# Mixture-of-experts stage: experts ranked on the chip, 14 units of 128 slots in place of 17

## The chip, the cores and the metric

The program runs on one core of one Trainium2 chip. The metric is device time in microseconds, the median over runs. Before the change it is 1516.67 us (three runs, 1516.6 to 1516.83).

## The reference

Two model blocks over 512 tokens of width 1024. The change lies in the first block's mixture of experts alone: a router picks one group of 8 experts for each token, then the two best of these 8. All 32 experts have three weight matrices of their own, 2 MB each in float32.

```python
g_idx = jnp.argmax(g_logits, axis=-1)                      # 4 groups
top_v, top_i = lax.top_k(e_logits, TOP_K_IN_GROUP)         # 2 of the group's 8
wts = g_prob[:, None] * jax.nn.softmax(top_v, axis=-1)
eid = (g_idx[:, None] * EXPERTS_PER_GROUP + top_i).reshape(-1)
...
def expert_block(args):
    tok_b, e = args
    xb = xpad[tok_b]
    h = jax.nn.silu(xb @ w_gate[e]) * (xb @ w_up[e])
    return h @ w_down[e]
```

512 tokens with two experts each are 1024 assignments, 32 for an expert on average. With the reference's inputs the counts of experts 4 to 31, in falling order, are 81, 69, 60, 53, 41, 41, 41, 39, 39, 36, 34, 33, 31, 31, 30, 27 and then twelve from 25 down to 10; experts 0 to 3 have 41, 44, 16 and 16.

## The kernel before

The program is one long instruction list per engine, written out by hand in Python; queues and engines run in the order of the text, with semaphores between them. SP issues nearly all loads, TensorE (PE) multiplies, DVE and ACT evacuate PSUM.

**Units.** The experts' work is cut into 17 units of 128 slots (`pair`, called at the end of the file's main loop, `for p in range(NPAIR + 1)`). A unit normally holds two experts with 64 slots each (`CAP`); each takes a 64-column tile of the PE array, and the two tiles' matmuls alternate (line 77 is the helper `mm`, which nearly all matmuls share). Units 8 and 12 (`DOUBLE`) hold one expert each, on both tiles: the two experts outside the first four with the most assignments, found on the chip. Assignments beyond an expert's slots go to extra units, up to 16 half units, inside a branch (`tc.If(n_more > 0)`, line 1344) after unit 5; with the inputs here the branch is not taken.

**A unit on PE.** Gate weights times gathered tokens, then up weights (`ld,XT`, 32 matmuls in the program; the chip runs float32 as two instructions, so the trace counts 64), then the previous unit's results are spread back to the tokens and added to `h` (`combine`, matmuls `O,oht`, in two halves around four transposes of `ms`), then, in every odd unit, the tokens of the next two units are gathered with one-hot matrices (`gathering`, 64 matmuls `og,hH` and `og,hL`), and then the down weights (`ld,ms`, 16 matmuls, 32 in the trace).

**Loads.** An expert's weights are six tiles `ld` of 1 MB (gate, up and down in two halves), 192 loads in all. `pump` puts them into SP's list as far ahead as the counters allow: at most `at["most"]` weight tiles that are not yet used (16 before the units, then 13, 11, 7 around the branch, 11, 9 for the last four), and 22 slots for all large tiles (`SLOTS`). SP then stands at a load until its slot is given up. From expert 4 on the source address comes from a table `xi` that DVE writes and SP reads into registers (`id_of`).

**Ranking.** `count_more` runs on DVE ahead of unit 0: from the counts `pr` it finds the two biggest experts, gives every assignment its slot `sl` and every place its expert `xi`. Unit 0's SiLU product (line 1061) and the rows `RW` of codes follow it on DVE.

**After the units.** `entering` adds the last unit's results and starts the second block: norm, transposes, and a split of the first weight tile on ACT (line 1267).

Of the kernel before, what the change touches and what calls it, by code (L numbers as in the profile page):

```python
# [20 lines left out]
S, D = 512, 1024  # L21
# [5 lines left out]
NPAIR = NE // 2  # L27
FIXED = 4
MORE = 5
DOUBLE = (8, 12)  # L30
# [3 lines left out]
TWICE = 16384.0  # L34
# [5 lines left out]
def kernel(  # L40
# [679 lines left out]
    places, at_place = {}, 0  # L720
    for p in range(NPAIR + 1):
        if p in DOUBLE:
            places[p] = (NE - 2 + DOUBLE.index(p),)
        else:
            places[p] = (at_place, at_place + 1)
            at_place += 2
        for n in range(3):
            for a in range(2):
                for i in places[p]:
                    jw[n, i, a] = want(partial(weights_of, n, i, a), [128, 4, 512], False)  # L730
# [23 lines left out]
    pcol = small([128, NPAIR + 1 + NEXTRA], "pcol", F32)  # L754
    P.iota(pcol, pattern=[[128, NPAIR + 1 + NEXTRA]], base=0, channel_multiplier=1, allow_small_or_imprecise_dtypes=True)
# [218 lines left out]
    wsl = small([128, 2, NPAIR + 1 + NEXTRA], "wsl")  # L974
# [52 lines left out]
    def pair(p, fetch, last=False, drop=False, own=None, after=None, tail=None):  # L1027

        X = XT[p // 2]
        off = (p % 2) * 128  # L1030
        if own is None:
            pair_codes(p)
        ahead = None
        if p % 2 and p < NPAIR:
            ahead = gathering(p // 2 + 1)
            next(ahead)

        def wfree(ws):
            if p <= NPAIR:
                n = len({id(w) for w in ws.values()})  # L1040
                wlive[0] -= n
                free(*[None] * n)
                pump()

        pg, pu = bank(), bank()
        for n, ps in enumerate((pg, pu)):
            for a in range(2):
                if own and n == 0:
                    next(own)
                ws = {(e, 0): fetch(n, e, a) for e in range(2)}  # L1050
                for k in range(4):
                    for e in range(2):
                        mm(ps[64 * e:64 * e + 64], X[:, 4 * a + k, off + 64 * e:off + 64 * e + 64],
                           ws[e, 0][:, k, :], a + k == 0, 4 * a + k == 7)
# [10 lines left out]
        if p - 1 in OT:  # L1065
            combine(p - 1, (0,))
# [5 lines left out]
        if p - 1 in OT:  # L1072
            combine(p - 1, (1,))
# [5 lines left out]
        for a in range(2):  # L1079
            ws = {(e, 0): fetch(2, e, a) for e in range(2)}  # L1080
            for half in range(2):
                for k in range(2):
                    f = (2 * a + k) * 128
                    for e in range(2):
                        mm(po[half][64 * e:64 * e + 64], ht[:, f + 64 * e:f + 64 * e + 64],
                           ws[e, 0][:, 2 * k + half, :], a + k == 0, a * k == 1)
# [24 lines left out]
    def listed(p):  # L1111
        one = {}

        def fetch(n, e, a):
            if e < len(places[p]):
                one[0] = moe_get(jw[n, places[p][e], a])
            return one[0]
# [6 lines left out]
    xbas, top = small([128, 2, NT], "xbas"), small([128, 8], "top")  # L1124

    def count_more():
        cnt, cand, onx, ony, tmp, tab, xb, xs_ = (wr[:, n, 0:NE] for n in range(8))
# [4 lines left out]
        V.memset(cand[:, 0:FIXED], 0.0)  # L1132
        for n, on in enumerate((onx, ony)):
            m, d = top[:, 0:1], top[:, 1 + n:2 + n]
            V.tensor_reduce(m, cand, axis=AX.X, op=OP.max)
            V.scalar_tensor_tensor(tmp, cand, m, dec, op0=OP.is_equal, op1=OP.mult)
            V.tensor_reduce(d, tmp, axis=AX.X, op=OP.max)
            V.tensor_scalar(on, dec, d, None, op0=OP.is_equal)
            if n == 0:
                V.scalar_tensor_tensor(cand, on, -BIG, cand, op0=OP.mult, op1=OP.add)  # L1140

        V.scalar_tensor_tensor(tab, dec, top[:, 1:2], place, op0=OP.is_lt, op1=OP.subtract)
        V.scalar_tensor_tensor(tab, dec, top[:, 2:3], tab, op0=OP.is_lt, op1=OP.add)
        V.tensor_scalar(tab, tab, -float(CAP), None, op0=OP.mult)
        for n, p in enumerate(DOUBLE):
            V.tensor_scalar(tmp, tab, float(2 * CAP * p), 2.0 * CAP, op0=OP.is_ge, op1=OP.mult)
            V.tensor_tensor(tab, tab, tmp, op=OP.add)
        for on, p in zip((onx, ony), DOUBLE):
            V.tensor_scalar(tmp, on, -1.0, 1.0, op0=OP.mult, op1=OP.add)
            V.tensor_tensor(tab, tab, tmp, op=OP.mult)  # L1150
            V.scalar_tensor_tensor(tab, on, float(2 * CAP * p + TWICE), tab, op0=OP.mult, op1=OP.add)

        V.tensor_tensor(tmp, onx, ony, op=OP.add)
        V.scalar_tensor_tensor(cnt, tmp, -float(CAP), cnt, op0=OP.mult, op1=OP.add)
        V.tensor_scalar(xb, cnt, float(CAP), None, op0=OP.is_gt)
        for n in range(2, S // CAP):
# [3 lines left out]

        V.tensor_tensor(top[:, 3:4], top[:, 1:2], top[:, 2:3], op=OP.max)
        V.tensor_tensor(top[:, 4:5], top[:, 1:2], top[:, 2:3], op=OP.min)
        V.tensor_scalar(top[:, 1:5], top[:, 1:5], -1.0, 100.0, op0=OP.mult, op1=OP.add)
# [625 lines left out]
```

## Time and profile before

| | us |
|---|---|
| median of three runs | 1516.67 |
| the profiled execution's own time | 1516.94 |
| its span in the trace | 1515.2 |
| PE busy in the span | 1461.1 |
| first expert matmul to last | 273.25 to 772.06 |
| the 192 expert loads issued | 202.33 to 741.4 |

The expert stage is about a third of the span. A row of a timeline or of the chain of waits gives start, length, engine, line, operation, and how many instructions are merged in it; `128*64` is the tile of the PE array. A row of busy time by stretch gives the stretch, its length, each engine's busy time, the granted PE clock (1.00 is 2.4 GHz, 0.50 is 1.2 GHz), the share of time that the DMA engines are busy, and the rate.

### The profile page before, as it was taken

Reading aid. Unit: us, or ns where it says so; the run is one execution under the profiler, and the core shown is the slowest. Engines: PE = TensorE matmul, PEld = TensorE weight load, DVE = VectorE, ACT = ScalarE, POOL = GpSimd, SP = SyncE. Lnnn points to the kernel's source line nnn. Section 1 sums busy time; section 2 is a strip of 40 time slices with the busy share of each in tenths; the row PEclk is TensorE's granted clock in tenths of the full one; section 3 lists DMA queues with packets and bytes.
Section 4 is the critical chain, followed back from the end, with each engine's and each line's share of the span. In section 5 each row is a group of like instructions: output and inputs, shape, how many; then the busy total and the mean of one; then the engine's idle time right before and its main releaser. Section 6 shows DMA issues by size and latency. Waiting matters only on the chain.

```text
span 1515.2 us, 20308 instructions
## 1 busy us (share of the span) xinstructions
PE 1461.1 (96%) x8135; PEld 1052.7 (69%) x8135; DVE 793.0 (52%) x1333; ACT 486.3 (32%) x706; POOL 185.8 (12%) x205
## 2 busy tenths in 40 slices
PE   6997999899999999999979999999999999999998
PEld 5876788454453553554548888889888888888876
DVE  5777746745243344244377656675445445444444
ACT  4434314311110111111134322223453453453442
POOL 1035304000000000000053000002202202102100
PEclk9998999999999999999989999999999999999999
DMA  8432563799979999979935564214113113113011
GB/s 307 173 129 94 172 261 135 289 380 422 421 289 407 422 421 419 420 297 368 416 118 194 171 218 139 98 44 152 56 57 112 56 57 112 56 56 112 29 70 56
DMA packets 102554, 310.69 MB, mean 205 GB/s; under 512 B 5120, under 2 KB 59028, under 8 KB 77876
## 3 DMA queue, kind: packets, MB, share of 16 engines
q1 hardware_dynamic: 94596, 281.36, 48.7%
q0 software_dynamic: 6704, 25.34, 4.7%
q10 hardware_dynamic: 1152, 2.62, 0.5%
q8 instruction: 66, 1.08, 0.3%
q14 instruction: 36, 0.29, 0.1%
HBM read 307.20 MB, written 2.10 MB: 204 GB/s over the span
## 4 chain that ended last, share of the span: by engine, by line
PE 67%; DVE 1%; POOL 1%; ACT 0%; issue 0%; POOLq 0%; DVEq 0%
PE ps L77 66%; PE ps L1618 1%; PE ps L393 0%; PE ps L1069 0%; POOL xs L1240 0%; PE ps L234 0%; DVE al L229 0%; DVE xs L1252 0%; DVE lo L115 0%; ACT hi L114 0%; POOL ss L1246 0%; POOL ss L1243 0%; DVE sq L1642 0%; DVE ms L1061 0%; POOL ss L1245 0%
## 5 line engine op out<-in xcount | busy, mean ns | idle before, releaser
L77 PE MATMUL ps<-ah,hi 128*128 128x512 f32 (+1 forms) x832 | 316.6, 381 | 0.4 <-ACT ah L245 0.4
L77 PE MATMUL ps<-al,hi 128*128 128x512 f32 (+1 forms) x832 | 311.1, 374 | 1.0 <-DVE al L229 1.0
L77 PE MATMUL ps<-ah,lo 128*128 128x512 f32 (+1 forms) x832 | 311.3, 374 | 0.0
L77 PE MATMUL ps<-ld,XT 128*64 128x512 f32 x1088 | 237.0, 592 | 2.1 <-DVEq L1344 1.9
L77 PEld LDWEIGHTS ps<-ld,XT 128*64 128x64 f32 x1088 | 81.3, 137 | 152.8 <-issue 149.2
L115 DVE TENSOR_TENSOR lo<-ld,hi 128x2048 fp32r<-128x2048 f32 (+1 forms) x71 | 160.9, 2272 | 47.0 <-ACT hi L114 47.0
L77 PEld LDWEIGHTS ps<-ah,hi 128*128 128x128 f32 x832 | 157.3, 189 | 29.5 <-issue 3.2
L77 PEld LDWEIGHTS ps<-ah,lo 128*128 128x128 f32 x832 | 157.1, 189 | 28.1
L77 PEld LDWEIGHTS ps<-al,hi 128*128 128x128 f32 x832 | 157.4, 189 | 27.4 <-DVE al L229 1.5
L77 PE MATMUL ps<-hi,ah 128*128 128x512 f32 (+1 forms) x456 | 170.2, 373 | 0.0
L77 PE MATMUL ps<-hi,al 128*128 128x512 f32 (+1 forms) x456 | 164.0, 360 | 0.0
L77 PE MATMUL ps<-lo,ah 128*128 128x512 f32 (+1 forms) x456 | 163.5, 359 | 0.0
L114 ACT ACTIVATE hi<-ld 128x2048 fp32r<-128x2048 f32 (+1 forms) x71 | 133.1, 1890 | 23.8 <-PE ps L77 16.0
L77 PE MATMUL ps<-ld,ms 128*64 128x512 f32 x544 | 122.2, 602 | 1.4 <-ACT ms L1070 1.4
L1091 DVE SCALAR_TENSOR_TENSOR O<-ps,wsl,O 128x512 fp32r<-128x512 f32 x34 | 25.4, 750 | 159.5 <-ACT O L1090 159.5
L1535 POOL TENSOR_TENSOR sq<-sq,rope 128x512 f32<-128x512 f32 x48 | 65.2, 1359 | 328.2 <-ACT sq L1533 328.2
L678 DVE TENSOR_TENSOR h<-h,ps 128x512 f32<-128x512 f32 x152 | 94.2, 678 | 12.8 <-PE ps L77 12.8
L77 PEld LDWEIGHTS ps<-hi,ah 128*128 128x128 f32 x456 | 86.9, 190 | 15.2 <-issue 4.0
L77 PEld LDWEIGHTS ps<-hi,al 128*128 128x128 f32 x456 | 86.8, 190 | 13.1
L77 PEld LDWEIGHTS ps<-lo,ah 128*128 128x128 f32 x456 | 87.1, 191 | 11.2
L77 PEld LDWEIGHTS ps<-ld,ms 128*64 128x64 f32 x544 | 38.0, 138 | 74.7 <-issue 70.0
L1534 DVE TENSOR_TENSOR qk<-ps,rope 128x512 f32<-128x512 f32 x48 | 33.2, 691 | 92.9 <-ACT sq L1533 92.9
(348 smaller groups left out, 1724.7 us busy)
## 6 DMA issues: line engine op xcount, KB each, us to landing
ld<-in_w_gate_dram SPq DMA_DIRECT2D x64, 1024.0 KB, 10.8
ld<-in_w_up_dram SPq DMA_DIRECT2D x64, 1024.0 KB, 12.1
ld<-in_w_down_dram SPq DMA_DIRECT2D x64, 1024.0 KB, 9.8
ld<-in_dil_w_in_dram SPq DMA_DIRECT2D x32, 1024.0 KB, 5.6
wm<-in_w_mod_dram POOLq DMA_DIRECT2D x24, 1024.0 KB, 5.6
ld<-in_conv_w_in_dram SPq DMA_DIRECT2D x16, 1024.0 KB, 11.0
ld<-in_w_in_dram SPq DMA_DIRECT2D x12, 1024.0 KB, 7.0
ld<-in_w_out_dram SPq DMA_DIRECT2D x4, 1024.0 KB
```

Of the source, the lines that this page charges most:

```text
L77: T.matmul(o, l, r, start=start, stop=stop)
L114: A.activation(hi[:, r], raw[:, r], AF.Copy)
L115: V.tensor_tensor(lo[:, r], raw[:, r], hi[:, r].bitcast(F32), op=OP.subtract)
L678: V.tensor_tensor(h[:, t, c * 512:(c + 1) * 512], h[:, t, c * 512:(c + 1) * 512], ps, op=OP.add)
L1091: V.scalar_tensor_tensor(OT[p][1][:, c], po[half], wsl[:, 0, p:p + 1], O[:, 0, c].bitcast(F32), op0=OP.mult, op1=OP.subtract)
L1534: V.tensor_tensor(dst, order(ps), order(rope[:, 0, :]), op=OP.mult)
L1535: P.tensor_tensor(sw, sw, rope[:, 1, :], op=OP.mult)
L1618: T.transpose(pt[:, j * 128:(j + 1) * 128], at_[:, i % 4, j * 128:(j + 1) * 128], ident)
```

## The change

The 28 experts after the first four are ranked by their number of assignments, on the chip. The two first get 128 slots each and a unit of their own, the next 14 get 64 slots, two to a unit as before, and the last 12 get 32 slots, four to a unit, each on a 32-column tile of the array. That makes 14 units. They run in the order `ORDER`: the two units of fixed experts, two units of four, two of two, the two with one expert, four of two, one of four, one of two. The branch for extra units stands after the fourth unit. All 192 loads remain.

```diff
 FIXED = 4
-MORE = 5
-DOUBLE = (8, 12)
+BIGS, MIDS = 2, 14
+UNITS = ([(0, 1), (2, 3), (4,), (5,)] + [(6 + 2 * n, 7 + 2 * n) for n in range(7)]
+         + [tuple(range(20 + 4 * n, 24 + 4 * n)) for n in range(3)])
+NU = len(UNITS)
+ORDER = (0, 1, 12, 13, 4, 5, 2, 3, 6, 7, 8, 9, 11, 10)
+MORE = 3
...
-        if p % 2 and p < NPAIR:
-            ahead = gathering(p // 2 + 1)
+        if then is not None:
+            ahead = gathering(then)
...
-                ws = {(e, 0): fetch(n, e, a) for e in range(2)}
+                ws = [fetch(n, e, a) for e in range(ne)]
                 for k in range(4):
-                    for e in range(2):
-                        mm(ps[64 * e:64 * e + 64], X[:, 4 * a + k, off + 64 * e:off + 64 * e + 64],
-                           ws[e, 0][:, k, :], a + k == 0, 4 * a + k == 7)
+                    for e in range(ne):
+                        mm(ps[w * e:w * e + w], X[:, 4 * a + k, off + w * e:off + w * e + w],
+                           ws[e][:, k, :], a + k == 0, 4 * a + k == 7)
                 wfree(ws)
...
-        V.tensor_scalar(cand, cnt, 1.0, None, op0=OP.add)
...
+        V.scalar_tensor_tensor(key, cnt, 64.0, dec, op0=OP.mult, op1=OP.add)
+        V.tensor_scalar(key[:, 0:FIXED], place[:, 0:FIXED], -1.0, -1.0, op0=OP.mult, op1=OP.add)
+        for n in range(2):
+            m = slice(16 * n, 16 * n + 16)
+            c3 = half().rearrange("p (a b) -> p a b", b=NE)
+            V.tensor_tensor(c3, spread_(key, 1, 16), spread_(key[:, m], 0, 16), op=OP.is_gt)
+            V.tensor_reduce(rank_[:, m], c3, axis=AX.X, op=OP.add)
...
+        V.tensor_scalar(cap, rank_, float(BIGS), float(CAP), op0=OP.is_lt, op1=OP.mult)
+        V.tensor_scalar(tmp, rank_, float(BIGS + MIDS), -CAP / 2.0, op0=OP.is_ge, op1=OP.mult)
+        V.scalar_tensor_tensor(cap, cap, float(CAP), tmp, op0=OP.add, op1=OP.add)
...
-        at["most"] = 11 if p < NPAIR - 4 else 9
-        if p == 3:
+            unit(u, listed(u), ne, p == NU - 1, p % 2, ORDER[p - 1], then, tail=entering if p == NU - 1 else None)
+        at["most"] = 11 if p < NU - 5 else 9
+        if p == MORE - 1:
             n_more = nc.values_load(xi[0:1, NE + 16:NE + 17], min_val=0, max_val=16)
-        if p == MORE - 1:
             at["most"] = 7
```

On PE, from the down weights of the second unit to those of the third, the list before the change is this (`ld` are weight tiles, `XT` gathered tokens, `ms` the product of the two projections, `O` a unit's results):

```order
L77 MATMUL ps<-ld,ms 64x512 x16
L77 MATMUL ps<-ld,XT 64x512 x32
L77 MATMUL ps<-O,oht 128x512 x8
L1069 MATMUL ps<-ident,ms 128x128 x4
L77 MATMUL ps<-O,oht 128x512 x8
L77 MATMUL ps<-ld,ms 64x512 x16
```

The same place of the changed kernel, in which `mm` stands on line 79:

```order
L79 MATMUL ps<-ld,ms 64x512 x16
L79 MATMUL ps<-ld,XT 32x512 x64
L79 MATMUL ps<-O,oht 128x512 x8
L1068 MATMUL ps<-ident,ms 128x128 x4
L79 MATMUL ps<-O,oht 128x512 x8
L79 MATMUL ps<-ld,ms 32x512 x32
```

The third unit has twice the matmuls, each on a tile of half the width; the spreading of results around them is as it was.

On DVE, the beginning of `count_more` before the change (`wr` holds its rows of 32, `top` the biggest two):

```order
L1129 COPY wr<-ps 128x32
L1131 TENSOR_SCALAR wr<-wr 128x32
L1132 MEMSET wr 128x4
L1135 TENSOR_REDUCE top<-wr 128x1
L1136 SCALAR_TENSOR_TENSOR wr<-wr,top,dec 128x32
L1137 TENSOR_REDUCE top<-wr 128x1
L1138 TENSOR_SCALAR wr<-dec,top 128x32
L1140 SCALAR_TENSOR_TENSOR wr<-wr 128x32
```

And now (`x` are scratch tiles, `io` a ramp):

```order
L1136 COPY wr<-ps 128x32
L1138 SCALAR_TENSOR_TENSOR wr<-wr,dec 128x32
L1139 TENSOR_SCALAR wr<-io_1526 128x4
L1143 TENSOR_TENSOR x_2007<-wr 128x512
L1144 TENSOR_REDUCE wr<-x_2007 128x16
L1143 TENSOR_TENSOR x_2010<-wr 128x512
L1144 TENSOR_REDUCE wr<-x_2010 128x16
L1149 TENSOR_TENSOR x_2013<-wr,io_1526 1x448
L1150 TENSOR_TENSOR x_2013<-x_2013,io_1526 1x448
L1151 TENSOR_REDUCE wr<-x_2013 1x14
```

The search for two maxima is replaced by a comparison of every count with every other, in two halves of 512 elements, and by the ranking's inverse in two halves of 448. The rest of `count_more` stays between the same neighbours on DVE, ahead of unit 0's SiLU product.

## Rows read from the trace of the kernel before

**Rows 1.** The page: busy engines, and DMA by slice of 37.9 us.

```profile
PE 1461.1 (96%) x8135; PEld 1052.7 (69%) x8135; DVE 793.0 (52%) x1333; ACT 486.3 (32%) x706; POOL 185.8 (12%) x205
...
DMA  8432563799979999979935564214113113113011
```

**Rows 2.** Busy time by stretch: length, PE, PEld, DVE, ACT, POOL, clock, DMA, GB/s.

```profile
340.00:442.00 102.00, 102.00 (x530) 51.53 (x528) 42.56 (x81) 16.40 (x30) 0.53 (x3) 1.00 1.01 420
442.00:455.00 13.00, 11.01 (x48) 4.86 (x44) 6.34 (x10) 1.49 (x3) 0.77 (x5) 1.00 0.12 35
455.00:644.00 189.00, 186.81 (x941) 90.55 (x942) 69.28 (x136) 27.43 (x49) 0.00 (x0) 0.99 1.01 418
644.00:686.00 42.00, 42.00 (x225) 22.43 (x225) 18.16 (x36) 7.50 (x14) 0.00 (x0) 1.00 0.70 276
686.00:752.00 66.00, 66.00 (x344) 31.76 (x342) 28.96 (x55) 11.75 (x22) 0.00 (x0) 1.00 1.00 413
```

**Rows 3.** The chain that ended last, units 10 and 11: start, us, what.

```profile
554.88 32.33 PE ps L77 x176
587.21 0.44 PE ps L1069 x4
587.65 24.64 PE ps L77 x112
612.29 0.44 PE ps L1069 x4
```

**Rows 4.** Timeline of PE: the branch, one unit, and the last matmuls.

```profile
441.53 7.09 PE L77 MATMUL ps<-ld,ms 128*64 128x512 f32 x32
...
455.33 14.21 PE L77 MATMUL ps<-ld,XT 128*64 128x512 f32 x64 [1.89 <-DVEq L1344]
...
506.51 7.09 PE L77 MATMUL ps<-ld,ms 128*64 128x512 f32 x32
513.43 13.90 PE L77 MATMUL ps<-ld,XT 128*64 128x512 f32 x64
...
764.97 7.09 PE L77 MATMUL ps<-ld,ms 128*64 128x512 f32 x32
```

**Rows 5.** Timeline of SP's issues: across the branch, and at the end.

```profile
426.19 27.63 SPq L96 DMA_DIRECT2D ld<-in_w_up_dram  x4
455.31 1.92 SPq L96 DMA_DIRECT2D ld<-in_w_down_dram  x4
...
739.38 2.04 SPq L96 DMA_DIRECT2D ld<-in_w_down_dram  x4
743.55 51.17 SPq L96 DMA_DIRECT2D ld<-in_conv_w_in_dram  x6
```

**Rows 6.** Timeline of PE in the second block's attention: tiles of 32 columns.

```profile
1125.39 1.48 PE L77 MATMUL ps<-zv,ident 128*32 128x256 f32 x24
```

**Rows 7.** Busy time by stretch, two stretches in which PE waited.

```profile
470.00:480.00 10.00, 8.59 (x34) 3.00 (x36) 0.66 (x1) 1.28 (x2) 0.00 (x0) 0.83 1.01 424
780.00:790.00 10.00, 3.27 (x13) 2.47 (x14) 8.47 (x6) 4.01 (x6) 9.63 (x9) 0.50 0.00 0
```

**Rows 8.** Timeline of DVE: `count_more` from first to last, and unit 0's product.

```profile
271.74 0.18 DVE L1129 COPY wr<-ps 128x32 f32<-128x32 f32 x1
...
280.90 0.67 DVE L1171 TENSOR_TENSOR x<-wr,io 1x512 f32<-1x512 f32 x1
281.60 0.67 DVE L1173 TENSOR_REDUCE wr<-x 1x16 f32<-1x512 f32 x1
...
286.43 0.17 DVE L1189 TENSOR_TENSOR sl<-sl,xbas 128x8 f32<-128x8 f32 x1
288.79 1.04 DVE L1061 TENSOR_TENSOR ms<-ms,ps 128x512 f32<-128x512 f32 x1 [2.19 <-PE ps L77]
```

**Rows 9.** Timeline of ACT behind the last expert matmul: the second block's first split.

```profile
772.69 1.90 ACT L1267 ACTIVATE hi<-ld 128x2048 fp32r<-128x2048 f32 x1
```

More of the change, by code (lines that the diff above doesn't have):

```diff
@@ L1025, in pair_codes, with unit @@
         OHT[p] = oht
-    def pair(p, fetch, last=False, drop=False, own=None, after=None, tail=None):
+    def unit(p, fetch, ne, last=False, drop=False, prev=None, then=None, own=None, after=None, tail=None):
         X = XT[p // 2]
         off = (p % 2) * 128
+        w = 128 // ne
         if own is None:
@@ L1079, in pair @@
         for a in range(2):
-            ws = {(e, 0): fetch(2, e, a) for e in range(2)}
+            ws = [fetch(2, e, a) for e in range(ne)]
             for half in range(2):
@@ L1123 @@
     xi = small([1, NE + 17], "xi", I32)
-    xbas, top = small([128, 2, NT], "xbas"), small([128, 8], "top")
     def count_more():
-        cnt, cand, onx, ony, tmp, tab, xb, xs_ = (wr[:, n, 0:NE] for n in range(8))
+        cnt, key, rank_, tab, cap, xb, xs_, tmp = (wr[:, n, 0:NE] for n in range(8))
         place = io256[:, 0:NE]
-        V.tensor_copy(cnt, pr[:, :NE])
-        V.tensor_scalar(cand, cnt, 1.0, None, op0=OP.add)
[L1132 to L1156, printed above, removed]
@@ new lines, in count_more @@
+        for n in range(2):
+            m = slice(NL // 2 * n, NL // 2 * (n + 1))
+            c3 = half()[0:1, :NL // 2 * NE].rearrange("p (a b) -> p a b", b=NE)
+            V.tensor_tensor(c3, spread_(rank_[0:1], 1, NL // 2), spread_(place[0:1, m], 0, NL // 2), op=OP.is_equal)
+            V.tensor_tensor(c3, c3, spread_(place[0:1], 1, NL // 2), op=OP.mult)
+            V.tensor_reduce(tmp[0:1, m], c3, axis=AX.X, op=OP.add)
+        V.tensor_copy(xi[:, FIXED:NE], tmp[0:1, 0:NL])
+        V.tensor_scalar(tab, rank_, 2.0 * CAP, 2.0 * CAP * FIXED / 2, op0=OP.mult, op1=OP.add)
@@ new lines, in count_more @@
+        for first, less in ((BIGS, CAP), (BIGS + MIDS, CAP // 2)):
+            V.tensor_scalar(tmp, rank_, -float(first), 0.0, op0=OP.add, op1=OP.max)
+            V.scalar_tensor_tensor(tab, tmp, -float(less), tab, op0=OP.mult, op1=OP.add)
+        V.tensor_scalar(tab[:, 0:FIXED], place[:, 0:FIXED], float(CAP), None, op0=OP.mult)
+        V.tensor_scalar(cap, rank_, float(BIGS), float(CAP), op0=OP.is_lt, op1=OP.mult)
+        V.tensor_scalar(tmp, rank_, float(BIGS + MIDS), -CAP / 2.0, op0=OP.is_ge, op1=OP.mult)
@@ L1205, in more @@
     def more(j):
-        gather((NPAIR + 1 + j) // 2)
-        pair(NPAIR + 1 + j, dynamic(j), True, True)
+        gather((NU + j) // 2)
+        unit(NU + j, dynamic(j), 2, True, True)
     def first_codes():
@@ L1321, in ev_conv @@
         return ev
-    for p in range(NPAIR + 1):
+    for p, u in enumerate(ORDER):
+        ne = max(2, len(UNITS[u]))
+        then = ORDER[p + 1] // 2 if p % 2 and p < NU - 1 else None
         if p == 0:
```

100 lines of the change are left out of this document (47 added, 53 removed).

## The prediction

> **What bounds the kernel now.** I read the page first: PE is busy 96% of the span and the DMA digits stand at 9 through the middle [rows 1], so two resources are candidates. The second look is busy time by stretch [rows 2]. From 340 to 442 us PE is busy all of the time and the DMA queue at share 1.01 moves 420 GB/s; a 1 MB load (1.0486 MB) takes 1.0486/0.420 = 2.50 us. 192 of them are 480 us, and the expert matmuls run from 273.25 to 772.06, 499 us: supply and demand are almost level. The chain of waits shows demand by unit [rows 3]: from 554.88 to 587.65 a unit with a gather, 32.8 us, and from there to the next, 0.44 us behind 612.29, one without, 25.1 us. Two units are 57.9 us of PE and, with two experts each, 24 loads, 60.0 us. PE is nowhere long idle, so before the change PE is the bound, but the queue is a few per cent behind it: whatever PE work goes, the loads are next.
>
> The last expert matmul ends at 764.97 + 7.09 = 772.06 [rows 4]. I write this end as a sum over the queue. In SP's list 79 of the 192 loads stand ahead of the branch, in either kernel; the queue runs dry at 442, when they are done, and 113 remain, 113 x 2.50 = 282.5 us, with about 1.2 us for the half-megabyte row that ACT loads in between. From the rates [rows 2], the queue idles 13 x (1 - 35/420) = 11.9 us at the branch, 42 x (1 - 276/420) = 14.4 us from 644 to 686, where the four last units' smaller look-ahead holds it, and 0.9 and 1.1 us in the other stretches: 28.3 us. So 442 + 282.5 + 1.2 + 28.3 = 754, and PE ends 18 us later: **before = 442 + 283.7 + 28.3 idle + 18 tail = 772.**
>
> **What the change removes: PE work.** 17 units become 14 and eight gathers behind the first become six: three times 25.1 and twice 7.7 (32.8 - 25.1), some 90 us. A unit of four experts has twice the matmuls, each on half the columns. Pairs take 13.90/64 = 0.217 us an instruction [rows 4]; a group, one half of one matrix, is 16 instructions and 3.5 us for two experts. For four it is 32, in 3.5 us if four tiles run side by side and 7.0 if two do. The nearest row decides: 24 instructions on 32-column tiles with 256 columns each take 1.48 us, of which the last one's drain is part, at most 0.062 each [rows 6]; for 512 columns at most 0.123 an instruction, 3.5 to 3.9 us a group. I take 3.5 and keep 7.0 as the far bound. None of these 90 us can be had in full, since the 480 us of loads stay.
>
> **The start.** Up to the third unit nothing changes but `count_more`. It takes 271.74 to 286.6, 14.9 us, and DVE is then idle 2.19 us before it needs unit 0's projections [rows 8]. The change puts in four operations of 512 elements at 0.70 us from start to start and six of 448 (0.61 each by size), 6.5 us, three products and sums over 256 elements in place of four over 128 (about even), and takes out some twenty small ones at about 0.2 us, 4 us. It ends 2.7 us later, 2.19 of which the idle time hides: **+0.5 us**, which goes through to the end, since the first loads wait for slots that PE gives up. If the broadcast comparison cost twice as much, it would be +3.3; less than 0 is excluded as far as the idle time hides a gain.
>
> **Third unit to the branch.** The third and fourth unit take 24 loads each, 60 us, for 25 and 33 us of PE. From the fourth group on PE waits for loads and the queue never waits for PE: every load in this stretch takes a slot given up a dozen loads earlier. So load 79 is done at 442 as before. Load 72, the fourth unit's last, is done at 442 - 7 x 2.5 = 424.5; with about 1 us to land and a group of 3.5 us PE is through at 429. Before, PE was through at 441.53 + 7.09 = 448.6, SP came over the branch at 426.19 + 27.63 - 0.35 = 453.5, 4.9 us later, and PE went on at 455.33, 6.7 us later [rows 4, 5]. Now SP is over at 434, when eight us of queued loads are still to run: **the 11.9 us of idle queue at the branch go to 0.** PE goes on at 436.
>
> **Branch to end.** Two units of two: 57.9 us and some 5 us of waits in which PE catches up with the queue, to 499; the queue then has load 102 and the next unit begins with 97. The two units of one expert take 57.9 us of PE for 12 loads, 30 us. Unhindered, the queue would be 16 loads ahead at 557. Of the 22 slots the two halves of `h` take 4, codes, gathered tokens, one-hots, products and results 6 or 7, so 11 or 12 are left for weights; the queue stops for about 4 loads, **10 us**. The four units of two behind them are level again, 115.8 us of PE against 120, but the queue now runs at the end of its slots, and I put **6 us** there (bounds 0 and the 14.4 that the same stretch idled before). PE comes to the last unit of four at 673, and the queue has about 28 loads to go; from there PE follows the loads: two more experts in the last unit, 5 us of loads for each 3.5 us pair of groups. The queue ends at 442 + 283.7 + 16 = 741.7. Behind that lie landing, the last group of 3.5 us, and a part of the spreading (4.6 us between up and down, of which PE has caught up most): **tail 5.5 us** in place of 18 (bounds 3.5 and 10).
>
> **The clock.** So far PE waits inside three units of four, and that is new. The rows show what waiting does: in 780 to 790 PE is busy 3.27 us and the granted clock is 0.50, the lower level of 1.2 GHz, after a stop of 5.6 us; in 470 to 480, behind two short stops, it is 0.83, a third of the stretch at the lower level [rows 7]. A group of 3.5 us in every 10 us of loads will meet it. A third of 10 us at half clock costs 1.7 us, a group then takes 5.2 us and still fits in 10; what is left over is the group before the branch, which shifts PE, and most of that is caught up again in the 5 us of waits. I put **+1.5 us** (bounds 0 and the rival below). The Trainium skill, "TensorE: Matmul & The Clock Gate", HAM oscillation, speaks against the change here: it says that a loop whose groups of matmuls each wait for a transfer falls back to the low clock before every group and pays for the ramp every time. The trace agrees that the clock falls behind stops, 0.50 and 0.83 [rows 7]; that it does so before every group no row shows. By that rule all of the groups in the units of four run slow, which is the second rival.
>
> **Behind the experts.** The second block's first split starts 0.6 us after the last matmul [rows 9] and its weights are next in SP's list, issued from 743.55 on [rows 5], 28 us ahead of use. They will come 2.5 and 5 us behind the last expert load at 741.7, so by about 747 with landing, as PE ends. It hides by a hair; without that cover it costs up to 3 us.
>
> **The sum.** 442 + 283.7 + 16 + 5.5 + 0.5 + 1.5 = 749 against 772: -23 us. The profiled execution took 1516.94 with a span of 1515.2; 1516.94 - 23 = 1493.9, and the median lies 0.3 below the profiled time, so **1493 us**, -1.6%.
>
> **Rivals.**
> 1. *The queue does not stop behind the branch.* The 16 us of idle are reckoned from slots, not seen. For: from 455 to 644, with the same two alternating units, it idled 0.9 us. Against: there PE took 12 loads in the time of one-expert units only once in four. With 3 us of idle it ends at 736, **1481**.
> 2. *All groups in the units of four run at the low clock.* For: 0.50 in [rows 7]. A group takes 7.0 us, still under 10, so the queue leads; but the fourth unit's last three groups end 3.5 us later each, the branch comes 10 us later, the queue idles 3 us there, and the chain to the end is some 8 us late: 757, **1501**. The same time holds if only two of the narrow tiles run side by side.
> 3. *The narrow tiles do not overlap*, and the change is slower. Place: the three units of four. A group of 32 instructions then takes 4 x 3.5 = 13.9 us, more than its 10 us of loads, and PE is the bound. With g for a group, the end is 332.8 (start of the third unit) + 18 g + 22 for the three units' spreading and gather + 6.7 for the branch + four pairs of 57.9 + 25.1 for the last = 618 + 18 g; it passes 772 at g = 8.6. At 13.9 it is 868, **1613**. For: no row has a 32-column tile with 512 columns that accumulates over eight steps. Against: [rows 6], three to four times under the price without overlap.
> 4. *More than the slots.* If an expert had more assignments than its rank's slots, the branch would be taken, and a pair of extra half units costs 33 us of PE and 30 us of loads that are not fetched ahead: slower by 10 to 40. The reference's counts exclude it: of the 28 ranked experts the second has 69, the third 60, the sixteenth 27 and the seventeenth 25.
>
> **How the numbers follow.** The forecast with its neighbours (1488 to 1498) 0.55; rival 1 and what lies around it (1477 to 1488) 0.17; rival 2 (1498 to 1507) 0.18; still faster but by less, to 1513, 0.03; about the same 0.03; rivals 3 and 4, slower, 0.04. A measurement of this kernel tells 0.2% (3 us) from no change; so faster 0.93, within 0.2% 0.03, slower 0.04. The range 1481 to 1503 holds the forecast, most of rival 1 and two thirds of rival 2.
>
> **What would show it.** In the trace after: PE idle in the third, fourth and next to last unit, with loads as releasers; the queue at share 1.0 across the branch; an idle stretch of the queue of about 10 us around 535 to 560; last expert matmul near 749 and within 6 us of the last load; narrow groups of 32 instructions in 3.5 us, or up to 7 with the clock at 0.5. The forecast is wrong if PE still ends 15 us behind the loads, if the queue's idle time exceeds 25 us, or if the time behind the last expert matmul grows.

## The result and the profile after

| | before | after |
|---|---|---|
| median, us | 1516.75 | 1497.97 |
| lowest to highest, us | 1516.60 to 1518.11 | 1496.25 to 1498.59 |
| the profiled execution, us | 1516.94 | 1498.59 |
| its span, us | 1515.2 | 1496.8 |
| last expert matmul ends | 772.06 | 752.82 |

The ratio of after to before is 0.9872, 95% interval 0.9855 to 0.9889: the change makes the kernel 1.3% faster, 18.8 us. The forecast was 1493, 23 us faster. The direction and the bound were right; the time is about 5 us longer than forecast, and the question of the experiments is where these 5 us are.

First the page of the kernel after: span, busy engines and DMA by slice (37.4 us each), and one group of expert matmuls with its idle time.

```profile
span 1496.8 us, 19787 instructions
...
PE   6997999898788999998879999999999999999998
...
DMA  8533553799999979999945654233203113113011
...
L79 PE MATMUL ps<-ld,XT 128*64 128x512 f32 (+1 forms) x1088 | 220.0, 618 | 30.8 <-DMA ld<-in_w_up_dram 17.5
```

PE now has slices under 9 in the expert stage, and most of this group's idle time there (17.5 of 30.8 us) ended with a load. That is the forecast's turn: the loads are next, and PE waits for them. Next, busy time by stretch of the kernel after (columns as in [rows 2]), cut where the queue's rate changes.

```profile
440.00:466.00 26.00, 23.76 (x100) 8.33 (x102) 4.46 (x9) 1.88 (x3) 0.00 (x0) 0.90 0.86 348
466.00:540.00 74.00, 70.47 (x350) 32.03 (x348) 30.38 (x63) 10.23 (x18) 0.00 (x0) 1.00 1.01 420
540.00:566.00 26.00, 26.00 (x150) 15.64 (x148) 9.72 (x16) 5.78 (x11) 0.00 (x0) 1.00 0.61 221
566.00:644.00 78.00, 78.00 (x392) 36.60 (x390) 29.61 (x58) 10.84 (x19) 0.00 (x0) 1.00 1.01 416
644.00:656.00 12.00, 12.00 (x66) 4.92 (x63) 4.14 (x6) 2.64 (x5) 0.00 (x0) 1.00 0.89 337
656.00:748.00 92.00, 80.60 (x446) 34.59 (x444) 30.51 (x59) 10.14 (x18) 0.00 (x0) 0.96 1.01 419
```

The queue stands below 420 GB/s in three places: at the branch, 26 x (1 - 348/420) = 4.5 us; behind the one-expert units, 26 x (1 - 221/420) = 12.3 us with PE busy all of the time; and 12 x (1 - 337/420) = 2.4 us at 644. From 656 on PE is idle for 11 us and the queue hardly at all (419 GB/s): the loads set the end.

The timeline of PE in the kernel after shows the narrow tiles, the branch and the end (the row at 455.33 of [rows 4] answers to the one at 440.35, the one at 764.97 to the one at 745.73).

```profile
421.61 8.13 PE L79 MATMUL ps<-ld,ms 128*32 128x512 f32 x64
...
440.35 16.33 PE L79 MATMUL ps<-ld,XT 128*64 128x512 f32 x64 [5.81 <-DVEq L1348]
...
679.61 7.92 PE L79 MATMUL ps<-ld,XT 128*32 128x512 f32 x70
687.91 3.74 PE L79 MATMUL ps<-ld,XT 128*32 128x512 f32 x28 [0.38 <-DMA ld<-in_w_up_dram]
693.10 1.04 PE L79 MATMUL ps<-ld,XT 128*32 128x512 f32 x2 [1.45 <-DMA ld<-in_w_up_dram]
695.58 1.04 PE L79 MATMUL ps<-ld,XT 128*32 128x512 f32 x2 [1.44 <-DMA ld<-in_w_up_dram]
698.06 5.15 PE L79 MATMUL ps<-ld,XT 128*32 128x512 f32 x26 [1.44 <-DMA ld<-in_w_up_dram]
...
745.73 7.09 PE L79 MATMUL ps<-ld,ms 128*64 128x512 f32 x32
```

70 narrow instructions take 7.92 us, 0.113 each, so 32 of them 3.6 us: four tiles do run side by side. Within a group the first instructions wait for the second and the third load one by one (693.10, 695.58), and the rest runs behind the fourth and last (698.06).

**What was not as forecast is the branch.** PE goes on at 440.35, not 436, and has waited 5.81 us. The instructions at the branch's line, 1348, in the kernel after (engine, operation, count, shortest, median and longest duration in ns, first and last start):

```profile
L1348 SPq EVENT_SEMAPHORE  x9: 17/17/17, 429.3 to 444.7; - x9
L1348 SPq COMPARE_BRANCH  x1: 53/53/53, 424.1 to 424.1; - x1
...
L1348 PEldq COMPARE_BRANCH  x1: 6092/6092/6092, 431.4 to 431.4; - x1
L1348 DVEq COMPARE_BRANCH  x1: 72/72/72, 434.6 to 434.6; - x1
...
L1348 DVEq EVENT_SEMAPHORE  x1: 21/21/21, 440.1 to 440.1; - x1
```

SP meets the branch at 424.1; the forecast had it over the branch at 434. It then runs nine semaphore instructions there, the last at 444.7. Each of eight of them waits for one semaphore of the load queue and adds to it what the skipped code would have added. From 434.8 on they come 2.4 to 2.5 us apart, the time of a load, because each sees one load landed. So SP issues nothing behind the branch until every load ahead of it has landed. The view of waits puts numbers to it: SP's queue (line waited in, what ended it: total us, times, longest), first after from 440 to 450, then before from 444 to 457.

```profile
SPq L1348 <- SPq L1348: 4.9, 2, 2.5
```

```profile
SPq L96 <- DVE O L1091: 4.8, 1, 4.8
SPq L96 <- PEq L1344: 3.6, 1, 3.6
SPq L1344 <- SPq L1344: 2.5, 1, 2.5
SPq L96 <- DVEq L1344: 1.2, 1, 1.2
```

Before, SP drained the queue in the same way (its semaphores there stand at 435.2 to 445.2), and behind that it waited for PE and DVE to give up a slot and to cross. The change took away this second part and left the drain.

The trace's records of packets give the ends of loads (a load of 1 MB is 128 packets of 8192 bytes; the end of the 79th is that of packet 79 x 128, whichever load that packet belongs to, so it says how much the queue has moved). They make the forecast's sum into a table. "Without the branch" is the first experiment below.

| term, us | before | forecast | after | without the branch |
|---|---|---|---|---|
| load 79 done | 444.7 | 442 | 444.2 | 442.2 |
| 113 loads at full rate | 283.7 | 283.7 | 283.7 | 283.7 |
| idle of the queue behind | 28.2 | 16 | 19.4 | 15.7 |
| last load to last matmul | 15.5 | 5.5 | 5.5 | 5.6 |
| start and clock, put on top | | 2 | | |
| last expert matmul ends | 772.1 | 749.2 | 752.8 | 747.2 |

### The profile page after: what moved, and what is told of

Read it like the earlier page. It is cut to its first block, busy times and chain, and to the rows that moved or that the text cites. A ratio compares the mean times of both kernels' runs of the same rounds, so it can differ in the third digit from the quotient of the medians.

```text
span 1496.8 us, 19787 instructions
## 1 busy us (share of the span) xinstructions
PE 1405.2 (94%) x7947; PEld 1006.2 (67%) x7947; DVE 758.8 (51%) x1248; ACT 470.9 (31%) x678; POOL 185.8 (12%) x205
## 4 chain that ended last, share of the span: by engine, by line
PE 62%; DMA 6%; DVE 1%; POOL 1%; issue 0%; ACT 0%; SPq 0%; POOLq 0%; DVEq 0%
PE ps L79 60%; DMA ld<-in_w_up_dram 4%; DMA ld<-in_w_down_dram 2%; PE ps L1622 1%; PE ps L395 0%; POOL xs L1243 0%; PE ps L236 0%; DVE al L231 0%; PE ps L1068 0%; DVE xs L1255 0%; DVE lo L117 0%; SPq L98 0%; ACT hi L116 0%; POOL ss L1249 0%; ACT O L1089 0%
## 5 line engine op out<-in xcount | busy, mean ns | idle before, releaser
L79 PE MATMUL ps<-ld,XT 128*64 128x512 f32 (+1 forms) x1088 | 220.0, 618 | 30.8 <-DMA ld<-in_w_up_dram 17.5
L79 PEld LDWEIGHTS ps<-ld,XT 128*64 128x64 f32 (+1 forms) x1088 | 65.9, 131 | 180.1 <-issue 129.9
L79 PE MATMUL ps<-ld,ms 128*64 128x512 f32 (+1 forms) x544 | 111.1, 626 | 9.7 <-DMA ld<-in_w_down_dram 8.3
L1090 DVE SCALAR_TENSOR_TENSOR O<-ps,wsl,O 128x512 fp32r<-128x512 f32 x28 | 20.9, 750 | 146.3 <-ACT O L1089 145.2
L1060 DVE TENSOR_TENSOR ms<-ms,ps 128x512 f32<-128x512 f32 x14 | 15.1, 1081 | 146.0 <-PE ps L79 104.9
L680 DVE TENSOR_TENSOR h<-h,ps 128x512 f32<-128x512 f32 x128 | 79.6, 679 | 12.8 <-PE ps L79 12.8
L79 PEld LDWEIGHTS ps<-ld,ms 128*64 128x64 f32 (+1 forms) x544 | 32.2, 132 | 79.6 <-issue 58.6
```

The costliest lines, as they stand in the source:

```text
L79: T.matmul(o, l, r, start=start, stop=stop)
L680: V.tensor_tensor(h[:, t, c * 512:(c + 1) * 512], h[:, t, c * 512:(c + 1) * 512], ps, op=OP.add)
L1060: V.tensor_tensor(prod.rearrange("p (j q) -> p q j", j=4), *(t.rearrange("p (q j) -> p q j", j=4) for t in (sil, pu)), op=OP.mult)
L1090: V.scalar_tensor_tensor(OT[p][1][:, c], po[half], wsl[:, 0, p:p + 1], O[:, 0, c].bitcast(F32), op0=OP.mult, op1=OP.subtract)
```

## The experiments

**1. Without the branch.** The units behind the branch and the branch are left out:

```
-            with tc.If(n_more > 0):
-                for j in range(NEXTRA):
-                    more(j)
```

> The branch and the extra half units behind it are left out (on these inputs they are not executed). Theory A, the branch costs the queue: SP has to see every load issued ahead of the branch landed before it issues the next, so the queue runs dry for about 4.5 us around 444, and PE waits 5.8 us for the jump. Without it the queue runs through 440 to 466 at about 420 GB/s (348 now), PE goes on at 436 rather than 440.35, and everything behind comes about 4 us earlier: last expert load done near 743, last expert matmul near 748.5, time near 1493.5. Rival B, the slots take it back: the stop behind the one-expert units (12.3 us now) grows by what the branch gave, the end moves by less than 1.5 us, 1497.

Measured: 1492.73 us (1491.12 to 1492.84), ratio to before 0.9837 [0.9821, 0.9853]; load 79 is done at 442.2, the last load at 741.6. The stretch at the branch in this kernel:

```profile
440.00:466.00 26.00, 22.14 (x96) 7.51 (x92) 6.82 (x15) 2.57 (x4) 0.00 (x0) 1.00 1.02 422
```

Where PE waited at the branch, its timeline now has no stop:

```profile
434.88 15.12 PE L79 MATMUL ps<-ld,XT 128*64 128x512 f32 x64
```

Theory A holds: the 5.2 us come through to the end. The column of the table says more. Without the branch the forecast's own numbers for the queue come out (442 and 442.2, 16 and 15.7, the end of the queue at 741.7 forecast and 741.6 measured), so the branch is what the sum was missing. The run takes out SP's drain and the crossings of PE and DVE together; that the drain is what the end feels rests on the idle time of the queue, and experiment 2 shows it by itself.

**2. Fewer loads ahead of the branch.**

```
-            at["most"] = 7
+            at["most"] = 2
```

> At the branch 2 loads are fetched ahead, not 7. Theory A, the drain: the queue loses the 4.5 us between the last landing ahead of the branch and the first packet behind it, however many loads stand ahead; only the place moves, to about 432, and PE and DVE jump while the queue is empty. So idle of 4 to 5 us again, last expert load done at 746 to 749, time within 2 us of 1498; the jump of PE takes about 3.4 us, as before the change, not 6.1. Rival B, the look-ahead hides most of the branch now: with 5 loads fewer ahead the queue idles 5 to 12 us more, and the end is that much later, 1503 to 1510.

Measured: 1498.04 us (1496.52 to 1499.45), the last load done at 746.2. The stretch of the drain, now earlier:

```profile
426.00:434.00 8.00, 7.49 (x57) 2.89 (x50) 2.88 (x5) 1.38 (x2) 0.54 (x4) 1.00 0.56 207
```

8 x (1 - 207/420) = 4.1 us of idle, where after has 4.5. The look-ahead at the branch hides nothing, because it is drained first: theory A holds, and rival B is refuted. This idle time lies before PE reaches the branch (432.7), so it is the drain's alone. The expectation for PE's jump failed: it took 6.3 us, not 3.4. But the queue was not empty during it, since SP was over the branch at 431.4 and loads ran again from 432.7 on, just as PE came to the branch (see the last section).

**3. Half of the loads in the units of four.** Two of the four experts' matrices are not loaded there; the other two are used twice.

```
-                for i in UNITS[u]:
+                for i in UNITS[u][:2]:
                     jw[n, i, a] = want(partial(weights_of, n, i, a), [128, 4, 512], False)
...
-            if e < len(UNITS[u]):
-                one[0] = moe_get(jw[n, UNITS[u][e], a])
-            return one[0]
+            if e < len(UNITS[u][:2]):
+                one[e] = moe_get(jw[n, UNITS[u][e], a])
+            return one[e % len(UNITS[u][:2])]
```

> The units of four fetch the weights of two of their experts alone and use them twice; the other two experts' matrices are not loaded, so 36 of 192 loads are left out, and nothing else. Theory A, the loads set the end of the experts: without 36 x 2.5 = 90 us of them PE is the bound again, its units cost 25.1 or 32.8 us, and the last expert matmul ends near 332.8 + 12 x 25.1 + 5 x 7.7 + 6.7 = 679, some 73 us earlier. Rival B, the narrow tiles or waits on PE itself set it: the units of four still take over 40 us each, and the end moves by less than 40 us.

Measured: 1428.76 us in one run. Three pieces of its chain of waits, each from one unit's transposes to the next unit's, and the last expert matmuls in its timeline. The first piece holds gate and up of a unit of two and a gather, the second gate and up of the last unit of four and a gather, the third the down weights of that unit of four:

```profile
440.46 32.32 PE ps L79 x176
...
616.01 32.46 PE ps L79 x240
...
648.90 24.79 PE ps L79 x144
```

```profile
675.90 7.09 PE L79 MATMUL ps<-ld,ms 128*64 128x512 f32 x32
```

Gate and up of a unit of four cost PE no more than those of a unit of two, 32.46 and 32.32 us, and the piece with its down weights takes 24.79, where [rows 3] has 24.64. The experts end at 682.99, 70 us ahead of after and 89 ahead of before: the "some 90 us" of PE work that the forecast took out are out, and 19 of them reach the end, since the loads hold the other 70.

**4. Narrow tiles not in turns.** Does the overlap of four tiles matter? The units of four issue their matmuls expert by expert:

```
+        def by(n):
+            if ne == 4:
+                return [(k, e) for e in range(ne) for k in range(n)]
+            return [(k, e) for k in range(n) for e in range(ne)]
...
-                for k in range(4):
-                    for e in range(ne):
...
+                for k, e in by(4):
...
-                for k in range(2):
+                for k, e in by(2):
```

> The changed kernel, with the matmuls of a unit of four issued expert by expert, not in turns, and nothing else. Theory A, tiles overlap only where neighbouring instructions stand on different column tiles: a group of 32 then takes four times its 3.5 us, 13.9 us, PE is the bound in the units of four, and the end comes at 618 + 18 x 13.9 = 868, time near 1613. Rival B, the order of issue does not matter or matters little: groups of 3.6 to 5 us, and the time stays within 5 us of 1498.

Measured: 1496.80 us in one run, last load done at 745.2. Gate and up of the third unit (128 instructions), which now changes tiles with every fourth matmul (eight instructions in the trace), then its down, which changes with every second:

```profile
331.71 29.82 PE L79 MATMUL ps<-ld,XT 128*32 128x512 f32 x128
...
365.80 7.14 PE L79 MATMUL ps<-ld,ms 128*32 128x512 f32 x64
```

29.82/4 = 7.5 us a group, so two tiles ran at a time; the instructions start in pairs, 0.43 us from pair to pair. That the pairs are the last of one expert and the first of the next fits, but the rows don't tell one tile from another. Theory A's price was twice too high, and B's "groups of 3.6 to 5 us" is wrong too; but B's time is right. A group of 7.5 us instead of 3.6 costs the end nothing, since 10 us of loads stand behind each.

**5. The clock.** PE is kept busy in its waits by matmuls that nothing reads, 16 of them behind a group in the first run, 4 in the second. They stand behind three of a unit's six groups: both groups of gate and the first of up. Behind the last of up and behind both groups of down there are none, though the expectation speaks of the down half too. The second run's edit:

```
+        def fill(ws):
+            if ne == 4:
+                pf = bank()
+                for k in range(4):
+                    mm(pf, X[:, k, off:off + 128], ws[0][:, k, :], k == 0, k == 3)
...
+                if not (n and a):
+                    fill(ws)
```

> The changed kernel with 16 more matmuls of 128 columns behind each group of a unit of four but the last of its up and of its down half (nothing reads their results), so that PE is busy for about 3.5 us of each wait for loads. Theory A, the low clock costs the end nothing, since the groups still fit into their 10 us of loads and the queue sets the end: the stretches at 0.50 between 363 and 401 and between 697 and 722 mostly go, the last expert load is done within 1 us of 747.3, time within 1.5 us of 1498. Rival B, the slow groups hold up the queue or the branch: the end comes 2 us or more earlier, below 1496.

Measured: 1557.92 us (1554.72 to 1557.99), a mistake of size that is worth its row:

```profile
332.87 56.15 PE L79 MATMUL ps<-ld,XT 128*32 128x512 f32 x224
```

128 of these are the unit's own, 128 x 0.113 = 14.5 us; 48 matmuls of 128 columns, two instructions each in the trace, took the other 41.6, 0.87 us each. I had taken the 0.217 of [rows 4], which is the time from one 64-column instruction to the next with two side by side. PE became the bound and the run says nothing on the clock. With 4:

> As the filled run before, with 4 matmuls of 128 columns behind a group in place of 16: there one took 0.87 us (41.6 us for 48 of them), four times what had been reckoned, so PE had become the bound. Now the filling takes 3.5 us of each 10 us of loads. Theory A, the low clock costs the end nothing, since the groups fit into their loads at either clock and the queue sets the end: the stretches at 0.50 between 363 and 401 and between 697 and 722 become shorter, last expert load done within 1.5 us of 747.3, time within 1.5 us of 1498. Rival B, the slow groups hold up the branch or the tail: 2 us or more earlier, below 1496.

Measured: 1496.68 us (1496.56 to 1498.37), ratio 0.9868 [0.9851, 0.9884]; last load done at 745.9. The last unit of four after, and in this run:

```profile
690.00:725.00 35.00, 26.78 (x136) 8.87 (x130) 7.50 (x12) 2.57 (x4) 0.00 (x0) 0.90 1.01 421
```

```profile
690.00:725.00 35.00, 31.86 (x182) 11.45 (x180) 10.10 (x18) 2.57 (x4) 0.00 (x0) 1.00 1.01 420
```

The clock is back at 1.00 there; one stretch at 0.50, from 373.6 to 380.5, stays ahead of the branch. The queue ends 1.4 us earlier, one trace against one. The time is 1.3 us lower, with intervals that overlap, so the times don't settle it; the size is within what theory A allows and under B's 2 us.

**6. The order of units.** Each one-expert unit behind a unit of four:

```
-ORDER = (0, 1, 12, 13, 4, 5, 2, 3, 6, 7, 8, 9, 11, 10)
+ORDER = (0, 1, 12, 2, 13, 3, 4, 5, 6, 7, 8, 9, 11, 10)
+THEN = {1: 6, 2: 1, 5: 2, 7: 3, 9: 4, 11: 5}
+DROP = (1, 4, 5, 7, 9, 11, 13)
...
-        then = ORDER[p + 1] // 2 if p % 2 and p < NU - 1 else None
+        then = THEN.get(p)
...
```

`THEN` says in which unit the tokens of a later pair are gathered, `DROP` behind which unit's gate and up a gathered tile is given up.

> The order of units alone: each one-expert unit behind a unit of four (0, 1, 12, 2, 13, 3, 4, ...), so the gathered tokens of two unit pairs are held at once for three units, one slot. Theory A, the stop of the queue behind the one-expert units comes from two of them in a row with 11 loads of look-ahead: apart they put PE 4 loads behind each, the unit of four takes that up, and the 12.3 us at 540 to 566 and the 2.4 us at 644 to 656 go. Last expert load done near 733, last expert matmul near 738, time near 1484. Rival B, the slot held longer and the gather inside the first unit of four stop the queue elsewhere: less than 5 us gained, over 1493.

Measured: 1488.71 us (1488.24 to 1489.18), ratio 0.9814 [0.9797, 0.9830]. The branch and all that follows it:

```profile
398.00:408.00 10.00, 6.49 (x30) 3.38 (x34) 8.29 (x16) 0.00 (x0) 0.17 (x1) 0.87 0.21 60
408.00:740.00 332.00, 303.50 (x1585) 132.53 (x1579) 105.86 (x201) 41.45 (x74) 0.00 (x0) 0.97 1.01 420
```

The stops behind the one-expert units are gone (420 GB/s to the end), as theory A has it, but the branch now costs 10 x (1 - 60/420) = 8.6 us, so the last load is done at 737.2, not 733, and the time lies between the two theories. The branch stands behind a one-expert unit here, and SP, the drain done, waits 4.3 us more for DVE to cross (from 396 to 410; the edit moves line 1348 to 1350 and the loads' line 98 to 100):

```profile
SPq L100 <- DVEq L1350: 4.3, 1, 4.3
```

Two runs moved the branch, `MORE = 4` and `MORE = 5`:

> The alternating order, with the branch one unit later, behind the second unit of four. Theory A, the price of the branch for the queue is the drain (4.5 us), and what it lost more in the alternating order (40 x (1 - 330/420) = 8.6 us at 380 to 420) is a wait for PE, which stood behind a one-expert unit there and freed slots late. Behind a unit of four PE has nothing left to free: idle of 4 to 5 us, last expert load done near 733, time near 1484.5. Rival B, two gathered tiles held at once take the slots wherever the branch stands: 8 us or more again, 1488.7 within 1.5.

> The alternating order, with the branch behind the second one-expert unit, where both of the gathered tiles held in between are free again. Theory A (a one-expert unit ahead of the branch puts PE behind, and the first load behind the branch waits for PE): the queue loses 8 us or more at the branch, time 1488 or more. Rival B (it was the slot of the second gathered tile): 4 to 5 us, time near 1484.5.

Measured: 1485.78 us (1484.87 to 1487.04, ratio 0.9793 [0.9776, 0.9809]) behind the unit of four, and 1494.94 us (1494.33 to 1496.43) behind the one-expert unit. The stretch of the branch in the one and in the other, and SP's waits there in the second, beside its drain:

```profile
450.00:470.00 20.00, 13.95 (x52) 6.08 (x53) 11.19 (x25) 0.60 (x1) 0.00 (x0) 0.83 0.78 314
```

```profile
470.00:490.00 20.00, 15.33 (x74) 8.00 (x75) 7.67 (x13) 3.04 (x6) 0.70 (x4) 0.97 0.38 140
```

```profile
SPq L100 <- DVE O L1092: 4.2, 1, 4.2
SPq L100 <- DVEq L1350: 3.5, 1, 3.5
SPq L100 <- PEq L1350: 3.5, 1, 3.5
```

5.0 us against 13.3. The price of a branch is the drain, plus what PE and DVE are late behind it: behind a unit of four, where PE waits for loads anyhow, hardly anything is added; behind a one-expert unit PE is late, and the loads wait for its slots. In both runs theory A holds.

**7. More look-ahead.** 13 loads in place of 11, from the fifth to the eighth unit:

```
-        at["most"] = 11 if p < NU - 5 else 9
+        at["most"] = 13 if 3 < p < 8 else 11 if p < NU - 5 else 9
```

> The changed kernel with 13 loads of look-ahead in place of 11 from the fifth to the eighth unit, nothing else. Theory A, the stop of the queue behind the one-expert units (12.3 us at 540 to 566) is the look-ahead's: each load more takes 2.5 us of it, so 7 us remain, the last expert load is done near 742, time near 1493. Rival B, the slots themselves are used up and the queue waits for a slot that something else than weights holds: the stop stays over 11 us, the time within 1.5 us of 1498.

Measured: 1497.22 us (1496.77 to 1498.43). Load 120 is done 9.0 us earlier than after (550.7 and 559.7), load 126 only 1.5 us (575.0 and 576.5), and the stretch of the stop is hardly better than the 221 GB/s above:

```profile
540.00:566.00 26.00, 26.00 (x150) 15.55 (x148) 10.11 (x18) 6.36 (x12) 0.00 (x0) 1.00 0.61 229
```

The queue stops later and as long: the gain is given back within the next six loads. The time is rival B's, its reason is not shown: SP's waits from 530 to 566 are for PE in both kernels (30.1 us, and 29.8 after), and whether a slot that something else holds is behind them was not tried. In the alternating order the same two loads, put into the first units:

```
+        at["most"] = 13 if p < 2 else 11 if p < NU - 5 else 9
```

> The alternating order with the branch behind the second unit of four, and 13 loads of look-ahead in place of 11 while the first three units run. Theory A, what is left to gain is the queue's idle time while the first two units run (44 x (1 - 347/420) = 7.6 us at 296 to 340): two loads more ahead take up to 5 us of it, and it is kept, since the units of four behind use up any look-ahead: last expert load done near 731, time near 1481. Rival B, given back as in the run with 13 loads in the middle units: the queue stops as much later, when the look-ahead returns to 11, time within 1.5 us of 1485.8.

Measured: 1484.97 us (1483.92 to 1485.52), ratio 0.9786 [0.9769, 0.9802]. The first two units, without and with it:

```profile
296.00:340.00 44.00, 44.00 (x274) 21.28 (x274) 20.53 (x45) 8.92 (x15) 0.00 (x0) 1.00 0.88 347
```

```profile
296.00:340.00 44.00, 44.00 (x268) 21.28 (x268) 19.22 (x42) 8.80 (x15) 0.00 (x0) 1.00 0.95 372
```

The queue gains 44 x (372 - 347)/420 = 2.6 us, half of what was expected, and keeps 2.1 to its end (733.6 and 735.7), one trace against one. That it is kept since PE waits for loads in the units of four behind it is argued, not shown. Theory A's 731 and 1481 are missed: the times differ by 0.8 us, which these runs can't tell from nothing and which is inside rival B's bounds.

**8. All together,** with the order of experiment 4:

> The run before last (alternating order, branch behind the second unit of four, 13 loads ahead in the first units) with the matmuls of a unit of four issued expert by expert. In the run with that order alone two of the four tiles overlapped (groups of about 7 us in place of 3.5) and the end came no later, since the loads set it, while the clock stayed at 1.00 through the units of four. Theory A: with PE busy for 7 of each 10 us of loads the stretches at 0.50 in the units of four go, which gives 1 to 2 us, time near 1483.5. Rival B: in this order a one-expert unit follows each unit of four at once, and slower groups put PE behind there: 1487 or more.

Measured: 1483.82 us (1483.75 to 1486.23), ratio 0.9786 [0.9772, 0.9799]. The stretches at 0.50 in the units of four are gone, as theory A has it (1.00 from 340 to 450 and from 640 on), and rival B's 1487 is not reached. But against experiment 7 there is no difference that can be measured, so theory A's gain of 1 to 2 us is not shown. Both versions are about 0.9% faster than the changed kernel and 2.1% than before.

## Why the prediction was right, and where 5 us went

**The bound.** Right. PE work goes, the loads are next: 89 us of PE work are gone, 19 us reach the end (experiment 3), and the last load is done 5.5 us ahead of the end of the last matmul, as forecast.

**The narrow tiles.** 3.5 to 3.9 us a group were forecast from [rows 6], 3.6 measured. Rival 3, no overlap, is refuted.

**The start.** Forecast +0.5, measured nothing. (Its terms, 6.5 - 4, make 2.5 us, not 2.7.) The last rows of `count_more` after, and unit 0's product, against [rows 8]:

```profile
288.06 0.17 DVE L1192 TENSOR_TENSOR sl<-sl,f 128x8 f32<-128x8 f32 x1
288.65 1.04 DVE L1060 TENSOR_TENSOR ms<-ms,ps 128x512 f32<-128x512 f32 x1 [0.43 <-PE ps L79]
```

`count_more` ends 1.6 us later, not 2.7, and 0.43 of the 2.19 us of idle time is left.

**Third unit to the branch.** Load 72 was forecast for 424.5 and is done at 424.53. Then comes the step that failed: "Now SP is over at 434, when eight us of queued loads are still to run: the 11.9 us of idle queue at the branch go to 0." I had read SP's lateness in [rows 5] as a wait for PE, 4.9 us behind PE's last matmul. It has two parts, the drain of the load queue and a wait for slots, and only the second has to do with PE. SP goes on at 444.7, and the branch costs 4.5 us instead of 0. Since the rate falls while the last load ahead of the branch is still running, 2.2 of them show as a later end of load 79 (444.2, not 442), the rest as idle time. PE's wait, 5.81 us in place of 1.89, is not the drain's: PE goes on at 440.35, when DVE is over the branch (434.6 to 440.1, where before had 453.5 to 455.1) and SP is not yet. PE's own jump took longer too (last section).

**Branch to end.** Idle time of 16 us was put there, 10 and 6; it was 12.3 behind the one-expert units and 2.4 at 644, with 1.0 in small losses (the two rates of 416 and 419), together 15.7. That the sum of 16 came out is partly luck: the first stop was put 2.3 us too low and the rest 2.6 too high. With the branch's part behind load 79 (4.5 - 2.2 = 2.3) that is 18.0 of the 19.4 in the table; 1.4 us I can't place. Rival 1, that the queue doesn't stop, is refuted for this order. Its 736 is an end of the experts (442 + 283.7 + 3 + 5.5 + 2), and no run with all loads reached it: in the alternating order, without those stops, they end at 741.2 with the branch behind the unit of four, and at 738.4 in experiment 8.

**The size of "before".** The tail before was written as 18 us behind the queue's end at 754. The packets show load 79 done at 444.7 and the last at 756.6, a tail of 15.5. The sum for before came out right by taking 2.5 us from the one term and giving them to the other, so the change looked 2.5 us better in the tail than it is.

**The clock.** The forecast's +1.5 fits the 1.4 us at the queue's end in experiment 5, but that is one trace against one, and the four executions of the changed kernel lie 2.3 us apart: the size is not shown. Outside of the branch the units of four show five stretches at 0.50 (from 363.3, 383.7, 394.0, 697.8 and 718.2 on). They fall on five of the 18 groups; in ten of the 18 the timeline has PE waiting for a load, and the five are among these. So the rule cited in the prediction from the Trainium skill, "TensorE: Matmul & The Clock Gate", HAM oscillation, holds for half of the groups that waited here, not for each. Rival 2's price was wrong as well: it had slow groups push the branch by 10 us, but the drain sets the branch, and experiment 4, with groups twice as long, ended no later.

**Behind the experts.** Forecast: hides by a hair. It is 1516.94 - 772.06 = 744.9 us before and 1498.59 - 752.82 = 745.8 after. The weights were there in time, as the first split follows its release at once:

```profile
753.45 1.90 ACT L1270 ACTIVATE hi<-ld 128x2048 fp32r<-128x2048 f32 x1
```

The 0.9 us stand beside a shift of the clock: a stretch at 0.50, equally long, lies there in both traces; it begins 2.5 us ahead of PE's first instruction of the second block in the one (780.0, 782.49) and 0.65 us ahead of it in the other (762.6, 763.25), so 1.8 us more of the second block's first matmuls run slow. No run changed that alone, but the kept traces go with it. From the last expert matmul to the end of the span it is 743.1 to 743.4 us in the three (before and both runs of experiment 5) in which the clock stays at 0.50 for 11.2 us behind that instruction, and 743.9 to 744.5 in the nine in which it stays there for 13.0 to 14.0. The filled runs have the changed code, so the code behind the experts is not the cause.

The 4.7 us by which the profiled execution misses 1493.9 are thus 3.6 us at the end of the experts, for which the branch alone would do, and 0.9 behind them, and rounding.

## What to carry to other kernels

Around a branch, ask what each engine that issues DMAs has to see landed before it may go on: look-ahead doesn't cover a drain, and the place to put a branch is one where the engine that frees the slots waits for loads anyhow. Where two resources are nearly level, order the work so that the stages that lean on one alternate with those that lean on the other: here that was worth 12 us without a byte or an instruction of work less. And check a sum at its joints (which load is done when) before its terms are moved, as one that closes only at the end can hide an error in two terms.

## What the runs showed that was not expected

**A jump takes longer while loads run.** PE's branch instruction took 3.3 to 3.7 us where the load queue stood idle and 5.9 to 6.3 us where loads were in flight. The first holds for five traces (before, experiment 3, the run with 16 filling matmuls, and the alternating order with the branch behind a one-expert unit, both times), the second for the other eight that have the branch. Three of these rows: before, experiment 2, and the last run of experiment 6.

```profile
L1344 PEldq COMPARE_BRANCH  x1: 3417/3417/3417, 450.3 to 450.3; - x1
```

```profile
L1348 PEldq COMPARE_BRANCH  x1: 6292/6292/6292, 432.7 to 432.7; - x1
```

```profile
L1350 PEldq COMPARE_BRANCH  x1: 3312/3312/3312, 481.3 to 481.3; - x1
```

The records of packets show where the difference lies. In each of the thirteen traces one packet of 16 KB on the queue named instruction falls into PE's branch instruction. It begins 0.9 to 1.1 us after PE meets the branch in the five and 3.4 to 3.9 us after it in the eight, takes 0.9 to 1.3 us in both, and PE goes on 1.3 to 1.5 us behind its end in both. So the longer jump is a later start of this packet; the loads take 96 to 99% of the DMA engines' time during the jump in the eight, and at most 5% in the five. That the packet is the code behind the jump is read from the name of its queue; no run tested it. The Trainium skill, "Runtime: NRT & Kernel Launch", Instruction fetch mechanics, says that a taken branch to code outside of what has been fetched ahead waits for a DMA of the target; the trace agrees that the jump waits for such a packet, and adds what it costs with the DMA engines idle and busy.

**Narrow tiles overlap without being issued in turns.** With four matmuls in a row on one 32-column tile (eight instructions in the trace), two tiles still ran at a time (7.5 us a group), and with two matmuls in a row all four did (7.14 us for two groups of down).
